# Holding DVE, ACT and POOL in the written order in the prompt-in, latents-out and prompt-out stages, and loading nine instead of five gated blocks early

## The chip, the core and the metric

The kernel runs on one core of one Trainium2 chip. The core has five engines with a queue of instructions each: TensorE (PE in the profile, with its weight loads as PEld), VectorE (DVE), ScalarE (ACT), GpSimd (POOL) and SyncE (SP), which here issues nearly all DMAs. [...] The metric is the device time of one execution in microseconds (us), as the median of several runs.

## The reference

One layer of a diffusion and flow-matching backbone is applied to two groups of tokens: 256 prompt tokens and 1024 latent tokens, of width 1024, in float32. Every step is modulated by vectors from a conditioning matrix product (`w_ada`).

```python
def swiglu(h, w_in, w_out):
    gate, up = jnp.split(h @ w_in, 2, axis=-1)
    return (jax.nn.silu(gate) * up) @ w_out
...
    h = rms_norm(x, p['norm_ffn1']) * (1.0 + sc1) + sh1
    x = x + 0.5 * g1 * swiglu(h, p['w_ffn1_in'], p['w_ffn1_out'])
    h = rms_norm(x, p['norm_mix']) * (1.0 + sc2) + sh2
    mix, k_ctx, v_ctx, s_ctx = token_mix(h, p, lb, lam_init, ctx_cache, rope)
    x = x + g2 * mix
    h = rms_norm(x, p['norm_ffn2']) * (1.0 + sc3) + sh3
    x = x + 0.5 * g3 * swiglu(h, p['w_ffn2_in'], p['w_ffn2_out'])
```

`token_mix` holds a gated linear recurrence and a differential attention. The two feed-forward networks (FFN1 and FFN2, inner width 2816 = 22 x 128) are what the change touches, with the first steps of the norms between them.

## The kernel before

**Matrix products.** Every float32 operand is split into two parts: a rounded high part (ACT, `copy`) and the rest (`tensor_tensor` with subtract, on DVE or POOL). A product is three matmuls: high by high, high by low, low by high. The tokens stand in three chunks: `CH[0]` and `CH[1]` of 512 latents each and `CH[2]` of 256 prompt tokens. For the latents the products of the FFNs use a seven-product scheme (Strassen with Winograd's sums) over quarters of the operands, so that sums of blocks have to be formed on DVE first.

**Stages of an FFN** (`ffn` in `build`), in order:

- `prompt_in`: the prompt tokens' gate and up products, 22 pairs of units of 24 matmuls. After each unit the next weight is split (`ahead(3)`: three units ahead, from four buffers) and `tick()` lets each generator in the list `side` take one step. There the latents' norms and their operands for the seven products (`operands`) are made, one step for each tick.
- `latents_in`: 11 x 2 x 7 products of the latents; gated blocks go to DRAM (`g_d`).
- `latents_out`: seven passes in the order `OUT = (1, 2, 5, 6, 7, 3, 4)`, each over 11 pairs of blocks: a weight block `b` and a gated block `g` of 128 x 512. `out_blocks` makes them: `self.block(a, .., G)` is an ACT cast and a POOL subtraction, `self.block(g, .., V)` an ACT cast and a DVE subtraction. In passes 5, 6, 7 and 3 a DVE sum comes first and the cast of `b` reads it. `pop(3)` makes blocks three ahead of the one in use; `wh` and `wl` have four buffers. After each block's 12 matmuls comes `tick()`: `drain` adds a pass's results into x (two `scalar_tensor_tensor` for each step; 16, 4, 8, 12, 8, 4 and 4 of them for the seven passes in order), and `later` takes one sum of squares for the next norm.
- `prompt_out`: 22 steps of 24 matmuls, two ticks for each; in FFN1 the norms of the two latent chunks (`norm` with `step=1`) run in its ticks.

**What sets the order.** The instructions are written in the order of the generators, and a planner then chooses each engine's order by its own estimate of when each instruction is ready; what is written first has priority. `keep_in_program_order` (line 51) takes that freedom away: an instruction it is called on stays behind the one written before it on the same engine. `nc.pin(names)` switches this on for the engines named and `nc.pin()` off. Before the change it is on only in attention (line 1681, for PE, DVE and ACT).

**Early loads.** `out_resident` loads weight blocks and five gated blocks (`g1`) into the space of the latents' operands (tags `hh0`, `hl0`, `hl1`), while `latents_in` ends. The gated blocks from the sixth on come through tag `gr` of the pool `op`, which takes the space of the pool `fp` of `latents_in`. Tags `hh2` and `hl2` hold the operand `t2` until the last product that reads it; then `out_resident` uses them for weights of pass 2.

Of the kernel before, what the change touches and what calls it, by code (L numbers as in the profile page):

```python
# [9 lines left out]
F32 = mybir.dt.float32  # L10
# [8 lines left out]
P = 128  # L19
# [14 lines left out]
def sub(a, off, dims):  # L34
    return bass.AP(tensor=a.tensor, offset=a.offset + off,
                   ap=[list(a.ap[0])] + [list(d) for d in dims])
# [29 lines left out]
class Kern:  # L66
# [9 lines left out]
    def pool(self, name, space=None, side=None):  # L76
        kw = {} if space is None else {"space": space}
        if space != DRAM:
            kw["reuse_waits"] = "tile"
        if side is not None:  # L80
            kw["side"] = side
        return self.tc.tile_pool(name=name, bufs=1, **kw)
# [273 lines left out]
    def rstd(self, tp, c, which, ms, lag):  # L356

        nc = self.nc
        n = CH[c][1]
        nt = n // P  # L360
        if ms is not None:
            nc.vector.tensor_tensor(ms[:, 0, :nt], ms[:, 0, :nt], ms[:, 1, :nt], op=ALU.add)
            ms = ms[:, 0]
        else:
            for _ in range(lag):
                yield
            acc, self.acc[c] = self.acc[c], {}
            ms = self.bank(f"pm{which}_{c}", nt)
            for t in range(nt):
                for h in range(2):  # L370
                    nc.tensor.matmul(ms[:, t:t + 1], acc[h][:, t * P:(t + 1) * P], self.ones[:, 0:1],
                                     start=h == 0, stop=h == 1)
        m = tp.tile([P, 4], F32, tag="nm", bufs=2, name=f"nm{which}_{c}")
        nc.vector.tensor_scalar(m[:, :nt], ms[:, :nt], 1.0 / D, EPS, op0=ALU.mult, op1=ALU.add)
        r = tp.tile([P, 4], F32, tag="nr", bufs=2, name=f"nr{which}_{c}")
        nc.gpsimd.tensor_tensor(r[:, :nt], m[:, :nt], self.nh[:, :nt], op=ALU.pow)
        dg = tp.tile([P, nt, P], F32, tag="t", bufs=self.tb, name=f"ndg{which}_{c}")
        nc.vector.tensor_tensor(dg, sub(self.ident, 0, [(0, nt), (1, P)]),
                                sub(r, 0, [(1, nt), (0, P)]), op=ALU.mult)
        yield  # L380
        if which:
            yield
        rb = self.bank(f"rb{which}_{c}", n)
        nc.tensor.matmul(rb, self.ones, dg.rearrange("p a b -> p (a b)"), start=True, stop=True)
        self.rb = rb
# [277 lines left out]

    def out_resident(self, hp, wout, name):

        t = [hp.tile([P, m, 512], F32, tag=g, name=f"{name}q{g}")
             for m, g in ((8, "hh0"), (8, "hl0"), (4, "hh2"), (2, "hl2"), (8, "hl1"))]
        fl = [x[:, j] for x, m in zip(t, (8, 8, 4, 2)) for j in range(m)]
        self.a11, self.a12 = fl[:NPR], fl[NPR:]
        self.s3, self.g1 = [t[4][:, j] for j in range(3)], [t[4][:, j] for j in range(3, 8)]  # L670
        for p in range(8):
            self.out_w(wout, self.a11[p], p, 0, 0)
            if p < 5:
                self.nc.sync.dma_start(self.g1[p], self.g_d[:, 0, p])

    def out_w(self, wout, t, p, i, j):
        self.nc.sync.dma_start(t, wout[0, (2 * p + j) * P:(2 * p + j + 1) * P, i * 512:(i + 1) * 512])
# [11 lines left out]
    def out_blocks(self, wout, name, hp, xp, pool):  # L689

        nc = self.nc
        V, G = nc.vector, nc.gpsimd
        keys = [(i, p) for i in self.OUT for p in range(NPR)]
        raws = {}
        xs = deque(self.x_pieces(xp))

        def load(j):
            if j >= len(keys):
                return
            i, p = keys[j]  # L700
            n_ = f"{name}w{i}_{p}"
            if j < 5:
                g = self.g1[j]
            else:
                g = pool().tile([P, 512], F32, tag="gr", bufs=4, name=n_ + "gr")
                nc.sync.dma_start(g, self.g_d[:, i - 1, p])
            a = None
            if i == 1:
                if p >= 8:
                    self.out_w(wout, self.a11[p], p, 0, 0)  # L710
            elif i == 2:
                self.out_w(wout, self.a12[p], p, 0, 1)
            elif i in (5, 7, 4):
                a = self.raw(pool, [P, 2, 512], n_ + "r")
                if i in (5, 7):
                    self.out_w(wout, a[:, 0], p, 1, 0)
                if i in (5, 4):
                    self.out_w(wout, a[:, 1], p, 1, 1)
            if xs and j >= 2 and j % 2 == 0:
                nc.sync.dma_start(*xs.popleft())  # L720
            if i == 5 and p == 4:
                self.x_move(pool(), 2, True)
            raws[j] = g, a
        s_ = None
        load(0)
        load(1)
        for j, (i, p) in enumerate(keys):
            load(j + 2)
            g, a = raws.pop(j)
            n_ = f"{name}w{i}_{p}"  # L730
            if i == 5 and p == 0:
                s_ = hp.tile([P, 8, 512], F32, tag="hh1", name=f"{name}s")
                s_ = [s_[:, q] for q in range(8)] + self.s3
            if i == 1:
                a = self.a11[p]
            elif i == 2:
                a = self.a12[p]
            elif i == 5:
                V.tensor_tensor(s_[p], a[:, 0], a[:, 1], op=ALU.add)
                a = s_[p]  # L740
            elif i == 6:
                V.tensor_tensor(s_[p], s_[p], self.a11[p], op=ALU.subtract)
                a = s_[p]
            elif i == 7:
                V.tensor_tensor(self.a11[p], self.a11[p], a[:, 0], op=ALU.subtract)
                a = self.a11[p]
            elif i == 3:
                V.tensor_tensor(self.a12[p], self.a12[p], s_[p], op=ALU.subtract)
                a = self.a12[p]
            else:  # L750
                a = a[:, 1]
            yield self.block(a, n_ + "b", G), self.block(g, n_ + "g", V)
# [747 lines left out]
def build(tc, ins, outs):  # L1500
    K = Kern(tc, ins, outs)
    nc = K.nc
# [4 lines left out]
    def mix_units():  # L1507
        K.tok_units(512, "hi0")
        for hd in range(4):
            K.hgrn_units(hd)  # L1510
            for w in MIX[hd]:
                K.tok_units(COL[w[0]] + 256 * int(w[1]), w)

    def ffn(st, name, which, hp, xp, side, nxt, done):

        win, wout = ins[f"w_{name}_in"], ins[f"w_{name}_out"]
        pool = {}
        ai, pi = K.stream(K.in_blocks(win, name, lambda: pool["fp"]))
        ao, po = K.stream(K.out_blocks(wout, name, hp, xp, lambda: pool["op"]))
        ap_, pp = K.stream(K.prompt_out_blocks(wout, name, lambda: pool["op"]))  # L1520

        def after():
            K.out_resident(hp, wout, name)
            ao(2)
        K.half = True
        K.xraw, K.nraw = st["raw"](), 3
        K.prompt_in(st["t"], name)
        K.finish_all()
        K.half = False
        K.xraw, K.nraw = None, 1  # L1530
        ai(1)
        st["close"]()
        with K.pool(name + "fp", side=side) as fp:
            pool["fp"] = fp
            st["side"]()
            K.latents_in(fp, name, pi, after)
            K.finish_all()
        st["end"]()
        with K.pool(name + "op", side=side) as op:
            pool["op"] = op  # L1540
            K.tb = 8
            m = 3 * which + 2
            K.latents_out(name, po, K.mt[m], K.ng[m], lambda c, d: done(op, c, d), lambda: ap_(2))
            K.prompt_out(name, pp, K.mt[m], lambda c, d: done(op, c, d))
            nxt(op)

    with ExitStack() as top:
# [7 lines left out]
        hp = top.enter_context(K.pool("h"))  # L1555
        K.ffn_units(ins["w_ffn1_in"], "ffn1")
        with K.pool("xx", side="right") as xp:
# [61 lines left out]
            def nxt(op):  # L1619
                mix_units()  # L1620
                K.ahead(2)
                ap = pv.enter_context(K.pool("pv"))
                K.att_consts(cp, ap)
                K.proj_v(ap, 0)
                K.finish_all()
                pv.close()
            ffn({"t": qp, "raw": lambda: qp, "close": q1.close, "side": lambda: K.side.append(adas()), "end": ta.close},
                "ffn1", 0, hp, xp, "right", nxt, done1)
        K.tb = 7
# [7 lines left out]
        for hd in range(4):  # L1637
            q = K.hgrn_q(gp, hd)
# [5 lines left out]
            for w in MIX[hd]:  # L1644
                g = int(w[1])
# [33 lines left out]
        with K.pool("atp", side="right") as atp, K.pool("psS", PSUM) as psS:  # L1679
# [3 lines left out]
            rest = [g for pr in (2, 3) for g in [K.proj_pair(avs[1][:2], *K.proj_av(att, 1), pr)] * 2]  # L1683
# [86 lines left out]
```

## Time and profile before

| what | us |
|---|---|
| runs (3), median | 2815.34 (2814.02 to 2816.27) |
| the profiled execution | 2819.1 |
| its span, first to last instruction | 2817.0 |
| PE busy | 2699.1 |
| DVE busy | 1666.7 |
| POOL busy | 1274.2 |
| ACT busy | 1116.4 |

The stages as the trace shows them, from the span's start: prompt-in of FFN1 to 193, its latents-in to 664, its latents-out 664 to 898, its prompt-out 898 to 978; the mixing to 1951; prompt-in of FFN2 to 2087, its latents-in to 2513, its latents-out 2513 to 2746, its prompt-out to 2811.

How to read it: every row has a start and a length, the engine, the operation with its tiles (`ffn1w_5g` is the split of gated block 5, `ffn1w_5b` that of weight block 5, `ffn1w_5gr` the raw gated block), and in brackets the idle time before and what ended it. A stage in which PE is busy all the time is bounded by PE; elsewhere the bracket names the engine that was late. All instructions are recorded by one helper (line 49), so the tile names tell them apart.

### The profile page before, as it was taken

Reading aid. Unit: us, or ns where it says so; the run is one execution under the profiler, and the core shown is the slowest. Engines: PE = TensorE matmul, PEld = TensorE weight load, DVE = VectorE, ACT = ScalarE, POOL = GpSimd, SP = SyncE. Lnnn points to the kernel's source line nnn. Section 1 sums busy time; section 2 is a strip of 40 time slices with the busy share of each in tenths; the row PEclk is TensorE's granted clock in tenths of the full one; section 3 lists DMA queues with packets and bytes.
Section 4 is the critical chain, followed back from the end, with each engine's and each line's share of the span. In section 5 each row is a group of like instructions: output and inputs, shape, how many; then the busy total and the mean of one; then the engine's idle time right before and its main releaser. Section 6 shows DMA issues by size and latency. Waiting matters only on the chain.

```text
span 2817.0 us, 43935 instructions
## 1 busy us (share of the span) xinstructions
PE 2699.1 (96%) x17070; PEld 2342.9 (83%) x17070; DVE 1666.7 (59%) x2158; ACT 1116.4 (40%) x1896; POOL 1274.2 (45%) x902
## 2 busy tenths in 40 slices
PE   7999999999899999999999899999999999999999
PEld 6986668887688889898989888888997888877789
DVE  3954446555876626464555488836745555557754
ACT  4642223333345523232323477745533333324344
POOL 2344334443545636455654112165454444435443
PEclk8999999999999999999999999999999999999999
DMA  9766663327635531313223954385653333257455
GB/s 302 232 187 213 203 203 121 106 83 242 231 119 187 175 123 58 109 61 101 67 81 99 224 116 104 121 282 162 187 150 102 96 102 113 94 190 253 135 178 185
DMA packets 412244, 429.29 MB, mean 152 GB/s; under 512 B 20620, under 2 KB 314756, under 8 KB 409988
## 3 DMA queue, kind: packets, MB, share of 16 engines
q1 hardware_dynamic: 411856, 426.43, 48.8%
q8 instruction: 134, 2.20, 0.3%
q14 instruction: 74, 0.61, 0.1%
q10 hardware_dynamic: 180, 0.06, 0.0%
HBM read 326.79 MB, written 99.61 MB: 151 GB/s over the span
## 4 chain that ended last, share of the span: by engine, by line
PE 80%; DVE 9%; DMA 4%; issue 3%; POOL 3%; SPq 1%; ACT 1%; ACTq 0%; DVEq 0%; POOLq 0%
PE ffn2po L49 6%; PE ffn1po L49 5%; PE mob L49 4%; PE ffn2pp L49 2%; PE ffn2pu L49 2%; PE ffn2pg L49 2%; PE ffn1pg L49 2%; PE ffn1pu L49 2%; PE ffn1pp L49 1%; PE ada L49 1%; PE ak1b L49 1%; PE ak0b L49 1%; PE aq0b L49 1%; SPq L49 1%; PE av1b L49 1%
## 5 line engine op out<-in xcount | busy, mean ns | idle before, releaser
L49 PE MATMUL ffn1pp<-ffn1pvv,ffn1pw 128*128 128x256 f32 x528 | 70.3, 296 | 5.6 <-DVE ffn1pvv L49 4.7
L49 PEld LDWEIGHTS ffn1pp<-ffn1pvv,ffn1pw 128*128 128x128 f32 x528 | 68.3, 203 | 7.5 <-DVE ffn1pvv L49 5.5
L49 PE MATMUL ffn2pp<-ffn2pvv,ffn2pw 128*128 128x256 f32 x528 | 64.0, 283 | 0.0
L49 PEld LDWEIGHTS ffn2pp<-ffn2pvv,ffn2pw 128*128 128x128 f32 x528 | 63.6, 192 | 0.1
L49 POOL TENSOR_TENSOR ffn2pw<-ffn2pw,ffn2pw 128x512 fp32r<-128x512 f32 x22 | 28.9, 1316 | 35.8 <-ACT ffn2pw L49 35.8
L49 PE MATMUL ada<-wada,cst 128*32 128x256 f32 x448 | 39.5, 391 | 0.6 <-DMA wada<-w_ada 0.5
L49 POOL TENSOR_TENSOR hl<-nt,hh 128x256 fp32r<-128x256 f32 (+1 forms) x20 | 22.3, 1119 | 39.0 <-ACT hh L49 36.6
L49 POOL TENSOR_TENSOR ffn1pw<-ffn1pw,ffn1pw 128x512 fp32r<-128x512 f32 x22 | 33.0, 1508 | 14.1 <-ACT ffn1pw L49 14.0
L49 ACT ACTIVATE nt<-nt,mt,sv 128x256 f32<-128x256 f32 (+1 forms) x40 | 25.7, 680 | 30.3 <-DVE sv L49 18.1
L49 DVE TENSOR_TENSOR sacc<-sacc,sq 128x512 f32<-128x512 f32 (+1 forms) x18 | 29.4, 1632 | 10.9 <-ACT sq L49 10.6
L49 PE MATMUL ffn1po<-ffn1w_5g,ffn1w_5b 128*128 128x512 f32 x84 | 24.4, 446 | 9.2 <-ACT ffn1w_5g L49 5.2
L49 ACT CAST ffn2pw<-ffn2pw 128x512 fp32r<-128x512 f32 x44 | 26.9, 620 | 15.5 <-PE ffn2pp L49 8.9
L49 ACT CAST ffn1pw<-ffn1pw 128x512 fp32r<-128x512 f32 x44 | 26.1, 616 | 16.3 <-DMA ffn1pw<-w_ffn_out 10.8
L49 DVE TENSOR_TENSOR ffn2pw<-ffn2pw,ffn2pw 128x512 fp32r<-128x512 f32 x22 | 16.9, 766 | 25.9 <-ACT ffn2pw L49 25.9
L49 PEld LDWEIGHTS ffn1po<-ffn1w_5g,ffn1w_5b 128*128 128x128 f32 x84 | 18.3, 220 | 14.1 <-ACT ffn1w_5g L49 5.6
L49 DVE TENSOR_REDUCE a_0mx<-a_0S 128x1 f32<-128x1536 f32 x8 | 14.1, 1757 | 24.3 <-PE a_0S L49 24.2
L49 PEld LDWEIGHTS ada<-wada,cst 128*32 128x32 f32 x448 | 9.6, 108 | 22.1 <-issue 19.5
L49 PE MATMUL ffn2po<-ffn2w_5g,ffn2w_5b 128*128 128x512 f32 x84 | 22.5, 421 | 5.6 <-ACT ffn2w_5g L49 5.6
L49 DVE TENSOR_TENSOR ffn1pw<-ffn1pw,ffn1pw 128x512 fp32r<-128x512 f32 x22 | 17.9, 816 | 13.2 <-ACT ffn1pw L49 13.2
L49 POOL TENSOR_TENSOR sacc<-sacc,sq 128x512 f32<-128x512 f32 (+1 forms) x18 | 25.0, 1392 | 0.5
L49 PEld LDWEIGHTS ffn2po<-ffn2w_5g,ffn2w_5b 128*128 128x128 f32 x84 | 17.0, 206 | 9.6 <-ACT ffn2w_5g L49 6.0
L49 PE MATMUL ffn2po<-ffn2w_9g,ffn2w_9b 128*128 128x512 f32 x84 | 22.0, 412 | 2.8 <-DVE ffn2w_9g L49 2.8
(4066 smaller groups left out, 10304.9 us busy)
## 6 DMA issues: line engine op xcount, KB each, us to landing
wada<-w_ada SPq DMA_DIRECT2D x112, 256.0 KB, 2.9
ffn1r<-w_ffn_in SPq DMA_DIRECT2D x44, 512.0 KB, 4.3
ffn2r<-w_ffn_in SPq DMA_DIRECT2D x44, 512.0 KB, 4.0
ffn1pw<-w_ffn_out SPq DMA_DIRECT2D x22, 512.0 KB, 3.4
ffn2pw<-w_ffn_out SPq DMA_DIRECT2D x22, 512.0 KB, 3.4
g_d<-ffn1t SPq DMA_DIRECT2D x33, 256.0 KB, 2.9
g_d<-ffn2t SPq DMA_DIRECT2D x33, 256.0 KB, 3.0
wadb<-w_ada SPq DMA_DIRECT2D x12, 512.0 KB, 9.1
```

Of the source, the lines that this page charges most:

```text
L49: r = f(*a, **k)
```

## The change

Three edits. `nc.pin("vector", "scalar", "gpsimd")` is switched on around `prompt_in` and around `latents_out` and `prompt_out` of both FFNs. `rstd` gets two more `yield`s: one between the row sums on PE and the DVE instruction that reads them, one (for the second and third norm) between the power on POOL and the DVE instruction that reads that; so each norm takes two ticks more. `out_resident` loads gated blocks 0 to 8 instead of 0 to 4, the four new ones into `hh2`; the last six weight blocks of pass 2, which had that space, get their tiles later (`rest12`, called in pass 2 at block 5).

```diff
@@ -370,10 +370,13 @@
                     nc.tensor.matmul(ms[:, t:t + 1], acc[h][:, t * P:(t + 1) * P], self.ones[:, 0:1],
                                      start=h == 0, stop=h == 1)
+            yield
         m = tp.tile([P, 4], F32, tag="nm", bufs=2, name=f"nm{which}_{c}")
         nc.vector.tensor_scalar(m[:, :nt], ms[:, :nt], 1.0 / D, EPS, op0=ALU.mult, op1=ALU.add)
         r = tp.tile([P, 4], F32, tag="nr", bufs=2, name=f"nr{which}_{c}")
         nc.gpsimd.tensor_tensor(r[:, :nt], m[:, :nt], self.nh[:, :nt], op=ALU.pow)
+        if which:
+            yield
         dg = tp.tile([P, nt, P], F32, tag="t", bufs=self.tb, name=f"ndg{which}_{c}")
@@ -663,15 +666,23 @@
     def out_resident(self, hp, wout, name):
 
-        t = [hp.tile([P, m, 512], F32, tag=g, name=f"{name}q{g}")
-             for m, g in ((8, "hh0"), (8, "hl0"), (4, "hh2"), (2, "hl2"), (8, "hl1"))]
-        fl = [x[:, j] for x, m in zip(t, (8, 8, 4, 2)) for j in range(m)]
+        def tile_(m, g, n="q"):
+            return hp.tile([P, m, 512], F32, tag=g, name=f"{name}{n}{g}")
+        t = [tile_(8, "hh0"), tile_(8, "hl0"), None, None, tile_(8, "hl1")]
+        fl = [x[:, j] for x in t[:2] for j in range(8)]
         self.a11, self.a12 = fl[:NPR], fl[NPR:]
-        self.s3, self.g1 = [t[4][:, j] for j in range(3)], [t[4][:, j] for j in range(3, 8)]
+        g = tile_(4, "hh2", "g")
+        self.g1 = [t[4][:, j] for j in range(3, 8)] + [g[:, j] for j in range(4)]
+
+        def rest():
+            t = tile_(4, "hh2"), tile_(2, "hl2")
+            self.a12 += [x[:, j] for x, m in zip(t, (4, 2)) for j in range(m)]
+        self.rest12 = rest
+        self.s3 = [t[4][:, j] for j in range(3)]
         for p in range(8):
             self.out_w(wout, self.a11[p], p, 0, 0)
-            if p < 5:
-                self.nc.sync.dma_start(self.g1[p], self.g_d[:, 0, p])
+            self.nc.sync.dma_start(self.g1[p], self.g_d[:, 0, p])
+        self.nc.sync.dma_start(self.g1[8], self.g_d[:, 0, 8])
@@ -699,7 +710,9 @@
             i, p = keys[j]
             n_ = f"{name}w{i}_{p}"
-            if j < 5:
+            if i == 2 and p == 5:
+                self.rest12()
+            if j < 9:
                 g = self.g1[j]
@@ -1524,8 +1537,10 @@
         K.xraw, K.nraw = st["raw"](), 3
+        nc.pin("vector", "scalar", "gpsimd")
         K.prompt_in(st["t"], name)
         K.finish_all()
+        nc.pin()
@@ -1540,8 +1555,10 @@
             m = 3 * which + 2
+            nc.pin("vector", "scalar", "gpsimd")
             K.latents_out(name, po, K.mt[m], K.ng[m], lambda c, d: done(op, c, d), lambda: ap_(2))
             K.prompt_out(name, pp, K.mt[m], lambda c, d: done(op, c, d))
+            nc.pin()
             nxt(op)
```

## The prediction

> **What bounds the kernel now.** I read the first table of the page, then busy time by stage, then PE's own timeline in the pinned stages, then the timelines of DVE, ACT and POOL around each idle time of PE.
>
> ```profile
> span 2817.0 us, 43935 instructions
> PE 2699.1 (96%) x17070; PEld 2342.9 (83%) x17070; DVE 1666.7 (59%) x2158; ACT 1116.4 (40%) x1896; POOL 1274.2 (45%) x902
> 55.77:193.00 137.23, 128.79 (x1018) 125.96 (x1018) 97.50 (x118) 81.19 (x135) 56.33 (x24) 0.96 0.73 219
> 658.50:980.00 321.50, 299.22 (x1536) 255.75 (x1535) 237.12 (x285) 145.09 (x260) 168.17 (x116) 0.97 0.59 194
> 1955.00:2112.00 157.00, 151.98 (x1150) 145.27 (x1148) 95.15 (x105) 72.81 (x106) 73.70 (x35) 0.99 0.59 170
> 2507.00:2730.00 223.00, 210.39 (x932) 172.77 (x931) 162.06 (x189) 86.91 (x153) 106.82 (x73) 0.98 0.60 195
> ```
>
> The last four rows are stretches: its bounds, its length, the busy time (and instructions) of PE, PEld, DVE, ACT and POOL, the granted clock, the DMA share, GB/s. PE is busy 96% of the span, so only its idle time and its slow clock can be won; whatever starves it is lost in full. In the four stages (prompt-in of FFN1, the out stages of FFN1, prompt-in of FFN2, latents-out of FFN2) its idle time is 8.4, 22.3, 5.0 and 12.6 us: some 48 us is the most that order can give, a little more with the clock that comes back late after a stop. In latents-out the idle time stands in two places.
>
> ```profile
> 658.77 0.39 PE L49 MATMUL ffn1u10p<-o0t2hh,ffn1w101s 128*128 128x512 f32 x1
> ...
> 675.31 2.88 PE L49 MATMUL ffn1po<-ffn1w_4g,ffn1w_4b 128*128 128x512 f32 x12
> ...
> 683.37 4.56 PE L49 MATMUL ffn1po<-ffn1w_5g,ffn1w_5b 128*128 128x512 f32 x12 [5.17 <-ACT ffn1w_5g L49]
> 687.76 2.90 PE L49 MATMUL ffn1po<-ffn1w_6g,ffn1w_6b 128*128 128x512 f32 x12
> ...
> 742.19 0.61 PE L49 MATMUL ffn1po<-ffn1w_4g,ffn1w_4b 128*128 128x512 f32 x2
> 746.04 2.56 PE L49 MATMUL ffn1po<-ffn1w_4g,ffn1w_4b 128*128 128x512 f32 x10 [3.23 <-POOL ffn1w_4b L49]
> 752.87 5.06 PE L49 MATMUL ffn1po<-ffn1w_5g,ffn1w_5b 128*128 128x512 f32 x11 [4.04 <-DVE ffn1w_5g L49]
> ...
> 777.23 0.39 PE L49 MATMUL ffn1po<-ffn1w_1g,ffn1w_1b 128*128 128x512 f32 x1
> ```
> ```profile
> 2523.94 2.88 PE L49 MATMUL ffn2po<-ffn2w_4g,ffn2w_4b 128*128 128x512 f32 x12
> 2532.44 4.99 PE L49 MATMUL ffn2po<-ffn2w_5g,ffn2w_5b 128*128 128x512 f32 x12 [5.61 <-ACT ffn2w_5g L49]
> 2537.26 2.88 PE L49 MATMUL ffn2po<-ffn2w_6g,ffn2w_6b 128*128 128x512 f32 x12
> ...
> 2586.22 0.39 PE L49 MATMUL ffn2po<-ffn2w_2g,ffn2w_2b 128*128 128x512 f32 x1
> ...
> 2593.79 2.98 PE L49 MATMUL ffn2po<-ffn2w_4g,ffn2w_4b 128*128 128x512 f32 x12
> ...
> 2619.53 2.91 PE L49 MATMUL ffn2po<-ffn2w_10g,ffn2w_10b 128*128 128x512 f32 x12
> ```
>
> Blocks that don't wait start 2.72 us apart. Blocks 4 and 5 of pass 1 take 687.76 - 675.31 = 12.45 us in FFN1 and 13.32 in FFN2, where two cost 5.44: 7.0 and 7.9 us are lost at gated block 5. In pass 5 eight blocks take 35.0 us in FFN1 (742.19 to 777.23) and 33.3 in FFN2, of which two groups of transposes take 1.6; eight cost 21.8: 13.3 and 10.0 us are lost while the planner has put sums for later passes ahead of the splits that PE needs.
>
> **The change part by part.**
>
> *Gated blocks.* Block 5 is late because its load comes so late:
>
> ```profile
> 656.47 2.22 SPq L49 DMA_DIRECT2D ffn1qhl<-g_d  x5
> ...
> 677.78 0.43 SPq L49 DMA_DIRECT2D ffn1w_5gr<-g_d  x1
> ```
>
> The five early loads issue at 656.47, the sixth only at 677.78. After the change blocks 5 to 8 load into `hh2`, whose last reader (t2) starts at 658.77, and block 9 is the first to wait for the pool: issued as late as block 5 was and landed 4.9 us later with its cast (682.70), it is needed only at 683.37 - 5.17 + 4 x 2.72 = 689.1. So -7.0 and -7.9. The same loads move forward on SP; weight blocks 6 and 7 queue behind them for at most 3 us and are needed after 680. `rest12` waits for gated blocks 5 to 8, used up a pass earlier: nothing.
>
> *The tail in front.* The first pinned DVE instruction (the split of gated block 2) now stands behind the last one of latents-in. That run of operations (the first and the last row), and PE's block 2:
>
> ```profile
> 663.80 0.68 DVE L49 TENSOR_TENSOR ffn1u10y<-ffn1u10x,ffn1u10p 128x512 f32<-128x512 f32 x1
> ...
> 675.75 0.68 DVE L49 TENSOR_TENSOR ffn1g10x<-ffn1t,ffn1g10z 128x512 f32<-128x512 f32 x1
> 669.87 2.88 PE L49 MATMUL ffn1po<-ffn1w_2g,ffn1w_2b 128*128 128x512 f32 x12
> ```
>
> From 663.80 twelve operations at 0.60 (one behind the other) end at 671.0, with one that meets POOL at 672; then the split, 0.69. PE wants it at 669.87: 1.8 to 2.9 us late, I take 2.5 for each FFN: +5.0.
>
> *Written order in passes 5, 6, 7 and 3.* For each block DVE's order is now: sum, split of `g`, two drains if there are any, next sum. The cast of `b` waits for the sum, the cast of `g` stands behind it on ACT, and DVE's split waits for that: a closed chain, where now the sums lie far ahead. Its pieces, from a steady stretch:
>
> ```profile
> 791.97 0.62 ACT L49 CAST ffn1w_9b<-ffn1qhl 128x512 fp32r<-128x512 f32 x1 [1.58 <-PE ffn1po L49]
> 792.49 0.62 ACT L49 CAST ffn1w_9g<-ffn1w_9gr 128x512 fp32r<-128x512 f32 x1
> 792.66 1.29 POOL L49 TENSOR_TENSOR ffn1w_9b<-ffn1qhl,ffn1w_9b 128x512 fp32r<-128x512 f32 x1 [1.42 <-ACT ffn1w_9b L49]
> 793.14 1.36 DVE L49 TENSOR_TENSOR ffn1w_9g<-ffn1w_9gr,ffn1w_9g 128x512 fp32r<-128x512 f32 x1 [1.35 <-ACT ffn1w_9g L49]
> 799.87 2.88 PE L49 MATMUL ffn1po<-ffn1w_9g,ffn1w_9b 128*128 128x512 f32 x12
> 755.14 0.68 DVE L49 TENSOR_TENSOR ffn1s<-ffn1s,ffn1qhh 128x512 f32<-128x512 f32 x1
> 779.95 2.06 DVE L49 SCALAR_TENSOR_TENSOR xr1a<-ffn1po,mt,xr1a 128x512 f32<-128x512 f32 x3
> ```
>
> From the start of `b`'s cast to the end of `g`'s split: 794.50 - 791.97 = 2.53 us; the split takes 1.36 instead of 0.69 because POOL's subtraction of `b` started before it. The sum adds 0.68 and a hand-over of some 0.05, less 0.1 by which successive DVE operations overlap: 3.15 us for each block against PE's 2.72. A drain adds 0.66 (three take 2.06). Behind the waiting split stand those drains and the next sum; ACT's next cast waits for the sum and PE for the split, so nothing runs ahead. For the 44 blocks: 44 x 3.15 = 138.6, and 32 drains (4, 8, 12, 8) x 0.66 = 21.1, together 159.7 against 44 x 2.72 = 119.7 us of PE: 40 too many. The start is covered: block 9 is ready at 794.50 and used at 799.87, 5.4 us of lead. So 34.6 us lost in FFN2; in FFN1 three POOL additions for the norm add 1.3 each, 38.5. Against 10.0 and 13.3 now that is +24.6 and +25.2. The trace doesn't show this chain closed, so bounds: drains hidden in the waits, 13.5 lost (44 x 0.43 - 5.4); no meeting with POOL, 5 lost; neither hidden and no lead, 44.
>
> *Prompt-in.* The same kind of chain stands in four of 22 steps (`operands`, c = 1): DVE difference, ACT cast, DVE split, twice, then the weights' split, then two more differences and a split.
>
> ```profile
> 109.24 0.69 DVE L49 TENSOR_TENSOR o0b<-x1b,o0a 128x512 f32<-128x512 f32 x1
> 110.78 1.22 DVE L49 TENSOR_TENSOR ffn1g10l<-ffn1g10r,ffn1g10h 128x1024 fp32r<-128x1024 f32 x1
> 165.71 2.41 POOL L49 TENSOR_TENSOR ffn1u18l<-ffn1u18r,ffn1u18h 128x1024 fp32r<-128x1024 f32 x1 [3.74 <-ACT ffn1u18h L49]
> ```
>
> Four waits for a cast and seven operations at 0.6, the weights 1.2 and 0.3 for the gate make 7.3 us for a step, and 8.8 if a POOL split (2.41) falls on DVE's work; PE needs 5.8. Four steps lose 6 to 12, less some 3 of lead: 3 to 9, I take 6 in each FFN. Idle now is 8.4 and 5.0: -2 and +1, with 2 more in FFN1 as my estimate for the slow clock behind its stops (-4), together -3; bounds -13 and +8.
>
> *Prompt-out and the yields.* In FFN1 the latents' norms run there:
>
> ```profile
> 900.00:910.00 10.00, 9.08 (x76) 8.87 (x75) 10.00 (x15) 7.59 (x15) 6.18 (x4) 1.00 0.63 226
> 930.00:940.00 10.00, 8.18 (x61) 7.58 (x62) 10.00 (x14) 7.83 (x17) 7.63 (x5) 1.00 0.44 127
> ```
>
> DVE is busy all the time here; the same work in another order ends no sooner. I put 0, with bounds of -8 (PE idles 2.74 us in these 20, so some 6 in the 43 us of the norms, and 2 in a stop near the stage's end) and +8 (half of the 16 steps wait 1 us for ACT). The yields move each norm back by two ticks, under 6 us, in stages where its reader comes later: 0.
>
> The sum: -14.9 + 5.0 + 49.8 - 3 + 0 = +36.9 us on the profiled execution's 2819.1 (span 2817.0 and 2.1 around it): 2856. The median lies 3.8 lower: 2852.
>
> **The rivals.**
>
> *The chain stays open (faster).* If the split doesn't meet POOL, a block costs 3.15 - 0.67 = 2.48 us, less than PE's 2.72, and only the drains are over: 109.1 + 21.1 - 119.7 - 5.4 = 5.1 lost, 9.0 in FFN1. The sum is -14.9 + 5.0 - 9.2 - 3 = -22, and -30 with prompt-out's 8: 2785 to 2793. It decides at 2.72 us for a block. For it: with a sum of DVE in front, POOL's timing may shift. Against it: all the steady splits in this stretch show 1.36. [...]
>
> *Drains hidden (no change).* They fall into waits for ACT: 13.5 and 17.4 lost, +7.6 instead of +49.8: 2810.
>
> *The clock falls (slower still).* PE now stops at every block.
>
> ```profile
> 750.00:760.00 10.00, 7.13 (x20) 5.68 (x21) 9.97 (x14) 1.14 (x2) 3.54 (x3) 0.66 0.46 141
> 760.00:770.00 10.00, 9.63 (x42) 7.31 (x40) 10.00 (x11) 3.56 (x7) 5.13 (x4) 1.00 0.52 175
> 973.26 4.51 PE L49 MATMUL ffn1pp<-ffn1pvv,ffn1pw 128*128 128x256 f32 x23 [2.07 <-DVE ffn1pvv L49]
> ```
>
> At a granted clock of 0.66 a block takes 4.1 us, the chain's mean is 3.63: 44 x 0.49 = 21.6 more in each FFN, 2895. For it: 0.66 after a stop of 4 us, and a slow restart after one of 2.07. Against it: 1.00 in 760 to 770, where PE still idles a little. [...]
>
> *The pins don't hold*: then only the gated blocks are left, -15: 2800.
>
> **How the numbers follow.** Forecast, the chain closed: 0.62, own range 2828 to 2880. Open chain: 0.19. Pins don't hold: 0.03. Drains hidden: 0.08. Clock falls: 0.08. A measurement tells about 0.2% from no change, 5.6 us. Slower 0.70, same 0.08, faster 0.22. The range 2786 to 2885 leaves out half of the faster cases and most of the clock's.
>
> **What would show it.** Right: PE's blocks in passes 5, 6, 7 and 3 start 3.1 us and more apart, some 4.5 with drains, each idle time ended by DVE's split of `g`; each cast of `b` right behind its sum; no stop at gated block 5, one of 2 to 3 us at block 2. Wrong: blocks at 2.72 in passes 6 and 7, or sums several blocks ahead of their casts.

## The result: slower by 3.46%, and the profile after

| | us |
|---|---|
| before, median of 5 runs in the comparison | 2815.34 (2811.69 to 2818.96) |
| after, median of 5 runs | 2912.24 (2909.93 to 2915.48) |
| ratio after to before | 1.0346, 95% interval 1.0334 to 1.0358 |
| forecast | 2852.0, range 2786 to 2885 |

The kernel became slower, as forecast, but by 96.9 us and not by 36.9: the time lies outside the range. The profiled execution's span went from 2817.0 to 2908.2, 91.2 us more; the profiled run of before lies 3.8 us above its median and that of after 2.3 below. First, busy time by stage, before and then after. A stage here goes from its first matmul to the first of the next one; the rows are prompt-in, latents-out and prompt-out of FFN1, prompt-in and latents-out of FFN2, with the columns as in the prediction (bounds, length, busy time of PE, PEld, DVE, ACT and POOL, granted clock, DMA share, GB/s).

```profile
35.00:192.70 157.70, 144.84 (x1124) 141.09 (x1125) 104.52 (x126) 92.15 (x154) 65.39 (x28) 0.95 0.75 222
664.40:897.80 233.40, 218.49 (x944) 178.00 (x943) 172.10 (x197) 95.99 (x170) 118.45 (x84) 0.98 0.59 195
897.80:977.80 80.00, 72.63 (x549) 70.67 (x548) 60.80 (x83) 45.78 (x86) 49.07 (x31) 0.94 0.55 181
1950.90:2086.30 135.40, 131.14 (x1075) 129.41 (x1074) 81.22 (x93) 67.44 (x95) 57.61 (x24) 0.99 0.62 183
2513.10:2745.50 232.40, 219.79 (x973) 180.56 (x972) 166.86 (x196) 91.43 (x162) 113.15 (x77) 0.98 0.60 195
```
```profile
34.90:207.80 172.90, 148.88 (x1124) 143.59 (x1125) 109.94 (x123) 91.61 (x154) 63.24 (x28) 0.92 0.66 203
679.60:940.30 260.70, 230.92 (x941) 172.29 (x941) 181.34 (x194) 94.22 (x168) 113.06 (x85) 0.99 0.53 173
940.30:1037.30 97.00, 77.57 (x550) 73.39 (x549) 66.18 (x86) 49.67 (x90) 47.18 (x33) 0.89 0.44 151
2008.40:2152.50 144.10, 135.24 (x1075) 133.53 (x1074) 91.08 (x104) 71.36 (x105) 59.26 (x25) 0.95 0.58 172
2580.20:2836.60 256.40, 230.55 (x973) 174.82 (x972) 178.54 (x195) 90.88 (x162) 101.21 (x78) 1.00 0.55 176
```

The five stages grew by 15.2, 27.3, 17.0, 8.7 and 24.0 us: 92.2, which is all of it (the rest fell by about 1). The two latents-out stages grew by 51.3, by the chain that was forecast; the forecast gave them +39.9 (-14.9 + 5.0 + 49.8). The two prompt-in stages and the prompt-out stage were forecast at -3 together and grew by 40.9: there the prediction failed. PE's busy time grew too, by 4.0, 4.9 and 4.1 us in the three prompt stages, with a granted clock of 0.92, 0.89 and 0.95 instead of 0.95, 0.94 and 0.99: the same matmuls ran longer behind the stops (a clock of 0.66 from 68 to 73 us, behind the first stop at `rb`; 0.50 from 956.3 to 964.3 in prompt-out; 0.50 from 2062.4 to 2068.4 in FFN2).

**Latents-out.** PE's own timeline in pass 6 of FFN1, first without drains, then with two drains for each block:

```profile
789.08 2.79 PE L49 MATMUL ffn1po<-ffn1w_2g,ffn1w_2b 128*128 128x512 f32 x11 [0.23 <-DVE ffn1w_2g L49]
792.33 2.79 PE L49 MATMUL ffn1po<-ffn1w_3g,ffn1w_3b 128*128 128x512 f32 x11 [0.23 <-DVE ffn1w_3g L49]
...
796.87 2.83 PE L49 MATMUL ffn1po<-ffn1w_4g,ffn1w_4b 128*128 128x512 f32 x11 [0.88 <-DVE ffn1w_4g L49]
...
801.42 2.79 PE L49 MATMUL ffn1po<-ffn1w_5g,ffn1w_5b 128*128 128x512 f32 x11 [0.88 <-DVE ffn1w_5g L49]
```

The blocks stand 3.25 us apart (792.33 - 789.08) and 4.55 with two drains (801.42 - 796.87); without a wait they stand 2.72 apart. Each stop ends with DVE's split of `g`. The engines beside it, from one block to the next (rows of the timeline of all engines, here and below in order of time):

```profile
789.74 0.62 ACT L49 CAST ffn1w_3b<-ffn1s 128x512 fp32r<-128x512 f32 x1 [2.10 <-DVE ffn1s L49]
...
790.26 0.62 ACT L49 CAST ffn1w_3g<-ffn1w_3gr 128x512 fp32r<-128x512 f32 x1
...
790.44 1.29 POOL L49 TENSOR_TENSOR ffn1w_3b<-ffn1s,ffn1w_3b 128x512 fp32r<-128x512 f32 x1 [1.96 <-ACT ffn1w_3b L49]
...
790.91 1.36 DVE L49 TENSOR_TENSOR ffn1w_3g<-ffn1w_3gr,ffn1w_3g 128x512 fp32r<-128x512 f32 x1 [1.28 <-ACT ffn1w_3g L49]
...
792.20 1.40 DVE L49 SCALAR_TENSOR_TENSOR xr1a<-ffn1po,mt,xr1a 128x512 f32<-128x512 f32 x2
...
793.52 0.67 DVE L49 TENSOR_TENSOR ffn1s<-ffn1s,ffn1qhh 128x512 f32<-128x512 f32 x1
...
794.30 0.62 ACT L49 CAST ffn1w_4b<-ffn1s 128x512 fp32r<-128x512 f32 x1 [3.42 <-DVE ffn1s L49]
```

Read in order of time: cast of `b` at 789.74, cast of `g` behind it, POOL's split of `b` at 790.44, DVE's split of `g` at 790.91 with 1.36 us because POOL started first (in e4, where DVE's split of `4g` comes first, it takes 0.68), two drains, the next sum at 793.52, and only then ACT's next cast of `b` (794.30), after 3.42 us of waiting for DVE. It is the closed chain.

**Prompt-out of FFN1**, where the latents' norms run in the ticks: PE, then DVE over one step.

```profile
986.61 0.74 PE L49 MATMUL ffn1pp<-ffn1pvv,ffn1pw 128*128 128x256 f32 x4 [1.49 <-ACT ffn1pvv L49]
988.94 2.65 PE L49 MATMUL ffn1pp<-ffn1pvv,ffn1pw 128*128 128x256 f32 x20 [1.59 <-DVE ffn1pvv L49]
993.09 0.74 PE L49 MATMUL ffn1pp<-ffn1pvv,ffn1pw 128*128 128x256 f32 x4 [1.50 <-ACT ffn1pvv L49]
```
```profile
988.81 1.27 DVE L49 TENSOR_TENSOR nt<-xr0b,rb 128x512 f32<-128x512 f32 x2
991.73 0.89 DVE L49 CAST hh<-nt 128x512 fp32r<-128x512 f32 x1 [1.65 <-ACT nt L49]
992.65 0.69 DVE L49 TENSOR_TENSOR hl<-nt,hh 128x512 fp32r<-128x512 f32 x1
993.26 1.76 DVE L49 TENSOR_TENSOR ffn1pw<-ffn1pw,ffn1pw 128x512 fp32r<-128x512 f32 x1
```

A step takes 993.09 - 986.61 = 6.48 us; its 24 matmuls take 3.39 (0.74 + 2.65). DVE multiplies two rows of the norm, then waits 1.65 us for ACT to scale and shift the second one, and only behind that cast and split does it come to the weights' split, which PE needs. Over the part of the stage in which the norms run, first before and then after (columns as in the stretches above):

```profile
897.80:939.00 41.20, 36.40 (x265) 34.91 (x264) 40.30 (x55) 29.30 (x55) 26.13 (x18) 0.92 0.47 156
940.30:1000.00 59.70, 43.70 (x288) 39.94 (x287) 43.05 (x58) 31.92 (x57) 24.60 (x19) 0.89 0.36 124
```

DVE was idle for 0.90 us of it (41.20 - 40.30) and is now for 16.65 (59.70 - 43.05). Nine waits for ACT's work on the norms make up 15.1 us of that; six of them are the wait of 1.65.

**Prompt-in.** In FFN1 PE stops at the broadcast of the norm (`rb`), in FFN2 at the weights of the steps in which the operands are made:

```profile
64.98 2.34 POOL L49 TENSOR_TENSOR ffn1u4l<-ffn1u4r,ffn1u4h 128x1024 fp32r<-128x1024 f32 x1
...
65.05 2.82 DVE L49 TENSOR_TENSOR ndg<-ident,nr 128x512 f32<-128x512 f32 x1 [1.13 <-POOL nr L49]
...
68.02 1.43 PE L49 MATMUL rb<-ndg,ones 128*128 128x512 f32 x2 [4.58 <-DVE ndg L49]
```
```profile
103.20 2.04 PE L49 MATMUL rb<-ndg,ones 128*128 128x512 f32 x2 [6.01 <-DVE ndg L49]
...
2060.22 2.84 POOL L49 TENSOR_TENSOR ffn2u8l<-ffn2u8r,ffn2u8h 128x1024 fp32r<-128x1024 f32 x1 [7.75 <-ACT ffn2u8h L49]
...
2060.78 2.83 DVE L49 TENSOR_TENSOR o2b<-xr1b,o2b 128x512 fp32r<-128x512 f32 x1
...
2063.12 0.58 PE L49 MATMUL ffn2pu<-hh,ffn2u8l 128*128 128x256 f32 x1 [2.42 <-POOL ffn2u8l L49]
...
2072.53 0.39 PE L49 MATMUL ffn2pu<-hh,ffn2u9l 128*128 128x256 f32 x1 [0.91 <-POOL ffn2u9l L49]
```

`ndg`, on which `rb` waits, takes 2.82 us, since POOL's split of the next weights started 0.07 us before it; in the two latents' norms PE stands still for 4.58 and 6.01 us. The meeting is 2.1 us of each (2.82 - 0.69). In FFN2 the steps with operands are 2072.53 - 2063.12 = 9.41 us long (the next two 9.38 and 9.40); the last DVE split of a step takes 2.83 us beside a POOL split that started 0.56 earlier.

### The profile page after: what moved, and what is told of

Read it like the earlier page. It is cut to its first block, busy times and chain, and to the rows that moved or that the text cites. A ratio compares the mean times of both kernels' runs of the same rounds, so it can differ in the third digit from the quotient of the medians.

```text
span 2908.2 us, 43948 instructions
## 1 busy us (share of the span) xinstructions
PE 2732.4 (94%) x17070; PEld 2337.6 (80%) x17070; DVE 1694.0 (58%) x2158; ACT 1113.1 (38%) x1896; POOL 1251.9 (43%) x902
## 5 line engine op out<-in xcount | busy, mean ns | idle before, releaser
L49 DVE TENSOR_TENSOR ffn2s<-ffn2s,ffn2pu 128x256 f32<-128x256 f32 x22 | 9.2, 416 | 42.5 <-PE ffn2pu L49 14.5
L49 DVE TENSOR_TENSOR ffn2pvv<-ffn2pv,ffn2pvv 128x256 fp32r<-128x256 f32 x22 | 12.8, 583 | 26.9 <-ACT ffn2pvv L49 26.5
L49 DVE TENSOR_TENSOR ffn1pw<-ffn1pw,ffn1pw 128x512 fp32r<-128x512 f32 x22 | 25.9, 1178 | 1.1 <-ACT ffn1pw L49 0.6
L49 PE MATMUL ffn1po<-ffn1w_6g,ffn1w_6b 128*128 128x512 f32 x84 | 21.8, 401 | 4.5 <-DVE ffn1w_6g L49 2.6
L49 PE MATMUL ffn1po<-ffn1w_2g,ffn1w_2b 128*128 128x512 f32 x84 | 22.5, 411 | 3.7 <-DVE ffn1w_2g L49 3.7
L49 PE MATMUL ffn1po<-ffn1w_7g,ffn1w_7b 128*128 128x512 f32 x84 | 21.8, 401 | 4.4 <-ACT ffn1w_7g L49 2.2
L49 PE MATMUL ffn2po<-ffn2w_6g,ffn2w_6b 128*128 128x512 f32 x84 | 21.9, 400 | 3.3 <-DVE ffn2w_6g L49 1.9
```

Source lines behind the costliest of these rows:

```text
L49: r = f(*a, **k)
```

## The experiments

All lengths by stage are from the first matmul of a stage to the first of the next, to within 0.2 us, in the profiled execution of each kernel (us):

| kernel | median | prompt-in 1 | latents-out 1 | prompt-out 1 | mixing | prompt-in 2 | latents-out 2 |
|---|---|---|---|---|---|---|---|
| before | 2815 to 2817 | 157.7 | 233.4 | 80.0 | 973.1 | 135.4 | 232.5 |
| after | 2912.2 | 172.9 | 260.7 | 97.0 | 971.0 | 144.1 | 256.4 |
| e1, gates alone | 2802.1 | 154.0 | 226.5 | 77.5 | 973.1 | 136.2 | 224.5 |
| e2, held in latents-out alone | 2876.2 | 155.7 | 260.0 | 79.5 | 978.4 | 135.5 | 257.1 |
| e3, sums one ahead | 2830.8 | 176.5 | 215.6 | 97.0 | 973.9 | 144.1 | 217.4 |
| e4, DVE alone held | 2835.5 | 161.8 | 228.3 | 94.9 | 981.5 | 141.9 | 224.3 |
| e8, ACT alone held | 2799.1 | 154.7 | 224.3 | 81.9 | 970.7 | 134.2 | 224.3 |
| e5, e3 + norms and operands ahead | 2815.8 | 169.9 | 217.3 | 91.3 | 973.8 | 139.8 | 218.0 |
| e9, e5 + weights split on POOL | 2815.9 | 167.4 | 214.0 | 87.6 | 976.5 | 139.8 | 217.6 |
| e6, e3 + rb later, hold later | 2813.4 | 164.2 | 211.3 | 95.9 | 971.6 | 144.1 | 214.8 |
| e10, all held, e3 + e5 + e6 | 2797.4 | 155.5 | 211.3 | 92.8 | 974.3 | 139.7 | 214.8 |
| e7, e2 + sums ahead, hold later | 2781.3 | 155.9 | 211.3 | 78.0 | 979.0 | 135.5 | 214.8 |

Prompt-in of FFN1 moves by up to 4 us between kernels that leave it alone, and the mixing by some 10: both are left out of the readings below where a difference is that small.

### e1: the nine gated blocks alone

```diff
-        nc.pin("vector", "scalar", "gpsimd")
         K.prompt_in(st["t"], name)
...
-            nc.pin("vector", "scalar", "gpsimd")
             K.latents_out(name, po, ...)
...
                                      start=h == 0, stop=h == 1)
-            yield
```

> The kernel before with the nine gated blocks alone: no engine held in the written order, no further yields. If the stop at gated block 5 comes from its late load alone, both stops (7.0 and 7.9 us) go and nothing else moves: 2815.3 - 14.9 = 2800. The rival: block 9 becomes the first late one and stops PE in its place, so that nothing is won: 2813 to 2817.

Measured: 2802.08, ratio 0.994 (0.9925 to 0.9955) to a before of 2816.94, so -14.9 us; latents-out 6.9 and 8.0 shorter. The stops at gated block 5 are gone and no other came in their place in pass 1. The term holds.

### e2: held in latents-out alone

```diff
-        nc.pin("vector", "scalar", "gpsimd")
         K.prompt_in(st["t"], name)
         K.finish_all()
-        nc.pin()
...
             K.latents_out(name, po, ...)
+            nc.pin()
             K.prompt_out(name, pp, ...)
-            nc.pin()
```

> The changed kernel, with the three engines held in the written order in latents-out alone (prompt-in and prompt-out are left to the planner; nine gates and yields stay). If each stage loses by its own written order, prompt-in gives back 15.1 + 8.7 us and prompt-out of FFN1 17.1: 2912.2 - 40.9 = 2871, with the out stages as long as in the changed kernel (260.7 and 256.4 us). The rival: the added yields, not the held order, cost the 17.1 us in prompt-out, which then stay: 2888.

Measured: 2876.24, ratio 1.0204 (1.0187 to 1.0221). Both prompt-in stages and prompt-out are back at their lengths of before (155.7, 135.5, 79.5) with the yields still in: the held order costs the 17 us there, the yields nothing. Latents-out stays as long as after the change. That the median is 5 above the forecast is the mixing (978.4), whose cause is not known.

### e3: the sum written one block ahead

```diff
             load(j + 2)
-            g, a = raws.pop(j)
+            while len(made) < min(2, len(keys) - j):
+                made.append(summed(j + len(made)))
+            a = made.popleft()
+            g, _ = raws.pop(j)
```

(`summed(j)` holds the lines that form block j's sum, unchanged.)

> The changed kernel with one thing moved in the written order: the DVE sum of a block is written one block ahead, before the split of the block in front of it. If the loss in passes 5, 6, 7 and 3 is the closed chain (sum, cast of b, cast of g, split), it opens: ACT's next cast of b no longer waits for the split. DVE then has 0.68 + 1.36 us for a block and 0.66 for each of 32 drains, a mean of 2.52 against PE's 2.72, so the blocks without drains stand 2.72 apart and most of 2 x 28 us goes: 2855 to 2865. The rival: DVE's meetings with POOL set the pace, not the chain; then the blocks stay 3.25 and 4.55 apart and the time stays within 5 us of 2912.

Measured: 2830.84, ratio 1.0043 (1.0027 to 1.0059): 81 us less than the change, and more than forecast. PE, ACT and DVE in pass 7 of this kernel:

```profile
802.50 0.68 DVE L49 TENSOR_TENSOR ffn1qhh<-ffn1qhh,ffn1w_1r 128x512 f32<-128x512 f32 x1
...
802.51 2.88 PE L49 MATMUL ffn1po<-ffn1w_8g,ffn1w_8b 128*128 128x512 f32 x12
...
802.75 0.62 ACT L49 CAST ffn1w_0b<-ffn1qhh 128x512 fp32r<-128x512 f32 x1 [1.58 <-POOL ffn1w_10b L49]
...
803.92 1.37 DVE L49 TENSOR_TENSOR ffn1w_0g<-ffn1w_0gr,ffn1w_0g 128x512 fp32r<-128x512 f32 x1 [0.75 <-ACT ffn1w_0g L49]
...
805.23 1.07 PE L49 MATMUL ffn1po<-ffn1w_9g,ffn1w_9b 128*128 128x512 f32 x4
```

The blocks stand 2.72 apart through all four passes, those with drains too (where transposes stand between them in FFN2 apart), though the split still takes 1.37 beside POOL. The sum at 802.50 is that of block 1 (it reads `1r`), while ACT has still to cast `0b`: the cast no longer waits for the newest sum. It seems to come as PE uses up blocks: its bracket names POOL's split of `10b`, but that had ended at 802.03, and the same wait of 1.58 before `8b`, `9b` and `10b` is put down to PE. So the chain set the pace; a meeting with POOL alone does not. More came back than forecast, because 2 x 28 us was the growth against the kernel before: against 2.72 us for each of 44 blocks the four passes had lost 44.4 and 41.9 us in the changed kernel, and now lose nothing in FFN1 and 3.6 in FFN2, which are the transposes.

### e4 and e8: one engine held

```diff
-nc.pin("vector", "scalar", "gpsimd")
+nc.pin("vector")
```

> The changed kernel with DVE alone held in the written order; ACT and POOL are the planner's. The closed chain needs both: ACT's cast of g behind the cast of b, and DVE's next sum behind the split of g. If ACT may cast g first, the split no longer waits for the sum: the out stages fall back from 260.7 and 256.4 us to about 235, some 45 us less, about 2865. The rival: DVE's order alone does the harm (whatever waits on it is late whichever way ACT goes); then 2895 to 2912.

> The changed kernel with ACT alone held in the written order. If the chain needs DVE's held order as much as ACT's, the planner puts the sums far ahead as before the change, the casts find them ready and the out stages come near those with the nine gates alone (226.5 and 224.5): about 2805. The rival: ACT's order alone, cast of g behind cast of b, does the harm: 2860 and more.

(e8 has `nc.pin("scalar")`.) Measured: 2835.45, ratio 1.0065 (1.0046 to 1.0083), and 2799.13, ratio 0.9951 (0.9933 to 0.9968). With DVE alone held, latents-out falls to 228.3 and 224.3. ACT and DVE where the planner uses ACT's freedom, in pass 6:

```profile
774.50 0.62 ACT L49 CAST ffn1w_3g<-ffn1w_3gr 128x512 fp32r<-128x512 f32 x1
...
775.02 0.62 ACT L49 CAST ffn1w_4g<-ffn1w_4gr 128x512 fp32r<-128x512 f32 x1
...
775.15 1.36 DVE L49 TENSOR_TENSOR ffn1w_3g<-ffn1w_3gr,ffn1w_3g 128x512 fp32r<-128x512 f32 x1 [1.28 <-ACT ffn1w_3g L49]
...
778.35 0.68 DVE L49 TENSOR_TENSOR ffn1w_4g<-ffn1w_4gr,ffn1w_4g 128x512 fp32r<-128x512 f32 x1
...
778.52 0.62 ACT L49 CAST ffn1w_4b<-ffn1s 128x512 fp32r<-128x512 f32 x1 [2.88 <-DVE ffn1s L49]
```

Up to 774.50 ACT goes in the written order and the split takes 1.36; the blocks there are 3.25 apart. At 775.02 the cast of `4g` comes ahead of that of `4b`: in blocks 4 to 7 the split of `g` is done before POOL starts on `b`, takes 0.68, and PE's blocks stand 2.72 apart from block 5 to the end of the pass. Where ACT is back in the written order, as at the start of pass 7, they stand 3.25 apart again. With ACT alone held the stages are about those of the gates alone. The chain needs the held order of DVE and of ACT; what holding POOL adds was not run by itself. Prompt-in of FFN2 and prompt-out are long with DVE alone held (141.9 and 94.9) and short with ACT alone (134.2 and 81.9): there it is DVE's order that costs.

### e5 and e9: the norms and the operands

```diff
+            while len(made) < (2 if step == 1 and d < KD - 1 else 1):
+                e = d + len(made)
...
+                nc.vector.tensor_tensor(t, self.x[c][e], rb, op=ALU.mult)
+                nc.scalar.activation(t, t, AF.Identity, ...)
+                made.append(t)
+            t = made.popleft()
...
-            self.split(t1[0][:, d], t1[1][:, d], a)
...
             nc.vector.tensor_tensor(b, x1[4 + d], a, op=ALU.subtract)
+            self.split(t1[0][:, d], t1[1][:, d], a)
```

> The kernel of e3 with two more places of the written order changed, each in a stage of its own: in prompt-out's norms the product and the ACT step of row d+1 are written ahead of the casts and splits of row d; in prompt-in's operands the second DVE difference is written ahead of the split of the first. If prompt-out loses by DVE's wait for ACT's step (1.65 us in each of some 5 steps of 6.48), the stage falls from 97.0 to about 88; in prompt-in one of the waits of 0.69 goes in four steps, 144.1 to about 141 in FFN2. The rival: DVE's own work with its meetings with POOL sets both stages (about 4.9 and 8.7 us for a step without any wait), so that the waits only fill room: both within 1 us of e3.

> The kernel of e5 with the first weight split of each prompt-out step moved from DVE to POOL, which then makes both. In e5 the steps with a norm in prompt-out of FFN1 stand 5.79 us apart and PE needs some 3.2. If what is left there is DVE's own work in the held order, lengthened by its meetings with POOL (split of the weights 1.1 to 1.76, of the gated block 1.49 instead of 0.41), the steps shorten by the 1.1 to 1.76 that leave DVE, until POOL is the bound: two splits and one for the norm, 3.9 us without meetings and 5.1 with them. Prompt-out of FFN1 from 91.3 to 84 to 88. The rival: the wait for ACT's casts sets the steps, whoever splits; then 91 and more, and POOL late in the steps without a norm too.

Measured: 2815.84, ratio 0.9998 (0.9986 to 1.001), and 2815.94, ratio 0.9998 (0.9987 to 1.001). In e5 prompt-out of FFN1 fell by 5.7 us (9 forecast) and prompt-in of FFN2 by 4.3 (3 forecast). PE's timeline in prompt-out of e5 and of e9:

```profile
941.71 2.65 PE L49 MATMUL ffn1pp<-ffn1pvv,ffn1pw 128*128 128x256 f32 x20 [0.99 <-DVE ffn1pvv L49]
...
947.50 2.65 PE L49 MATMUL ffn1pp<-ffn1pvv,ffn1pw 128*128 128x256 f32 x20 [0.98 <-DVE ffn1pvv L49]
```
```profile
931.82 2.64 PE L49 MATMUL ffn1pp<-ffn1pvv,ffn1pw 128*128 128x256 f32 x20 [0.53 <-DVE ffn1pvv L49]
...
937.15 4.75 PE L49 MATMUL ffn1pp<-ffn1pvv,ffn1pw 128*128 128x256 f32 x25 [0.53 <-DVE ffn1pvv L49]
```

The steps went from 6.48 to 5.79 in e5 and to 5.33 in e9, where prompt-out fell by 3.7 us more. Both theories hold a part. In e5 DVE waits 0.35 us a step for ACT's row of the norm and 0.58 for its cast of the weights, together 0.93 instead of 1.65: 0.7 us less, as the step. In e9 the split of 1.1 has left DVE, but its waits for ACT are 0.35 and 1.40 (now for the cast of the gated block), 0.8 more than in e5, so that the step is only some 0.5 shorter. The 1.9 us that e9 still has over PE's 3.39 are PE's stops for ACT's cast of the gated block (1.42) and for DVE's split of it (0.53); no run takes them out.

### e6: rb one tick later, the hold from the second block on

```diff
         yield
-        if which:
+        if which or more:
             yield
         rb = self.bank(f"rb{which}_{c}", n)
...
+                if i == 1 and p == 1:
+                    nc.pin("vector", "scalar", "gpsimd")
                 w, v = pop(3)
```

(`more` is true for the latents' first norms.)

> The kernel of e3 with two edits: the broadcast of the latents' first norms (rb) is written one tick later, and the three engines are held in the written order from the second block of latents-out on, not from its start. If rb stands in PE's queue a tick too early for a DVE that is held in order, its two stops (4.48 and 6.02 us) go, and with them some 2 us of slow clock: prompt-in of FFN1 from 176.5 to about 164. If the split of block 2 is late because it stands behind the tail of latents-in, its stops (2.46 and 2.32 us) go too: latents-out 213 and 215 us. In all about 2815. The rival: the norm's result is late whenever it is asked for, so that the stops move to its readers, and block 2 waits for its load: 2830.

Measured: 2813.36, ratio 0.9994 (0.9982 to 1.0006). Prompt-in of FFN1 is 164.2, as forecast (8.7 us shorter than after the change, 12.3 than in e3): one stop at `rb` is 1.75 us, the other is gone. Latents-out is 211.3 and 214.8, and PE does not stop there at all: the stop at block 2 was the tail in front.

### e7 and e10: put together

e7 has the gates, the held order in latents-out alone and from its second block on, and the sums one block ahead. e10 holds all stages, as the change does, with the edits of e3, e5 and e6.

> What the stages so far suggest together: nine gated blocks; the three engines held in the written order in latents-out alone, from its second block on; the sums written one block ahead. From the stages: 2815.3 - (233.4 - 213.2) - (232.5 - 215.1) = 2778. The rival: prompt-in and prompt-out, left to the planner, or the mixing come out longer than before (they did by 5 us in e2): 2785.

> All three stages held in the written order as in the change, with every edit of that order from e3, e5 and e6 together: the sums one block ahead, the norm's rows one ahead, the operands' differences first, rb one tick later, the hold of latents-out from its second block on. If each closed a wait of its own, they add up: from e3 (2830.8) 12.3 for rb, 4.3 + 2.6 for block 2, 5.7 for the norms, 4.3 and some 4 for the operands: 2798, faster than before, though every stage is still held. The rival: the planner's freedom is worth something that no written order here gives back; the gains overlap and it stays at 2808 to 2815.

Measured: e7 2781.34 (2779.10 to 2786.73), ratio 0.9884 (0.9865 to 0.9903): faster than both kernels, by 34 us than before (2815.74 beside it) and by 131 than after. It lies between the two cases because the mixing is 979.0 instead of 973.1. e10: 2797.44, ratio 0.9928 (0.9911 to 0.9945), as forecast: the gains of the edits add up to within a few us in each stage. So most of the cost was not that the order was held but which order it was. Not all of it: with every edit prompt-out still takes 92.8 us against 80.0 before and prompt-in of FFN2 139.7 against 135.4, and e7, which leaves both to the planner, is 16 us faster than e10.

## Why the prediction was wrong

**Gated blocks, -14.9**: right. e1 gives -14.9.

**The tail in front, +5.0**: right in mechanism, too small; +8.2. Blocks 2 of the first passes:

```profile
686.63 1.63 DVE L49 TENSOR_TENSOR ffn1g10x<-ffn1t,ffn1g10z 128x512 f32<-128x512 f32 x1
...
688.92 3.45 PE L49 MATMUL ffn1po<-ffn1w_2g,ffn1w_2b 128*128 128x512 f32 x9 [3.00 <-DVE ffn1w_2g L49]
...
2589.47 2.33 PE L49 MATMUL ffn2po<-ffn2w_2g,ffn2w_2b 128*128 128x512 f32 x9 [2.96 <-DVE ffn2w_2g L49]
```

The stops are 3.00 and 2.96 us, where 1.8 to 2.9 were forecast: two of the tail's operations met POOL in each FFN (1.67 and 1.63 us instead of 0.68), where one was counted. With the slow clock behind the first (0.66 from 689 to 694 us), pass 1 of FFN1 lost 4.9 us there (blocks 2 and 3 from 685.08 to 695.47, less 5.44) and that of FFN2 3.3 (2585.66 to 2591.64, less 2.72).

**Written order in passes 5, 6, 7 and 3, +49.8**: right; +58.8. A block took 3.25 us (forecast 3.15), a drain 0.65 (4.55 - 3.25, halved; forecast 0.66). From the first block of pass 5 to that of pass 4, FFN1 went from 133.8 us (731.31 to 865.15) to 164.1 (744.43 to 908.54) and FFN2 from 133.0 (2580.78 to 2713.82) to 161.6 (2643.32 to 2804.93). In the forecast's own sum 0.10 us more in each of 88 blocks are 8.8 of the 9.0 by which the term was too small. The first blocks of pass 5 still start 2.72 apart, on the lead that the sum allowed for; in passes 6 and 7 what would have shown it wrong, blocks at 2.72 or sums several blocks ahead of their casts, is not there. The rival of the hidden drains fell, and so did that of the falling clock: between these stops it was granted in full (1.00 over the four passes, 744.43 to 908.54 and 2643.32 to 2804.93 us).

**Prompt-in, -3 (bounds -13 and +8)**: wrong; +23.9. Two things went wrong in the step. It priced the operands' chain at 7.3 us for a step, 8.8 with a meeting; it measured 9.41, since the meeting at its end costs 2.83 - 0.69 = 2.1 us and not 1.5 (7.3 + 2.1 = 9.4; the 7.3 comes out though the step has two waits of 0.69 for a cast, where four were counted), and the slow clock behind the new stops was not in the sum. And it counted only the operands: the norms of the same generator, held in the same order, were left out. By the rows of the result, 10.6 of the 23.9 us are the two stops at `rb`, 8.1 the busy time that PE gained at the slower clock (4.0 + 4.1), and 5.2 other idle time. The stops at `rb` and the clock behind them are most of the 15.2 us in FFN1: with `rb` later the stage is 8.7 us shorter than after the change and 12.3 shorter than in e3, which the edit starts from (e6).

**Prompt-out, 0 (bounds -8 and +8)**: wrong; +17.0. The step read: DVE is busy all the time here, the same work in another order ends no sooner. That is true and says nothing of how much later it ends. A DVE without idle time has no room to take in a wait: the held order put 15.1 us of waits for ACT in its way, and PE's idle time over the same part grew from 4.80 to 16.00 us. The bound of +8 took a wait of 1 us in half of the 16 steps; six waits of 1.65 and three others came, and PE's matmuls ran 4.9 us longer at the slower clock. Where e5 took 0.7 us of wait out of a step, the step became 0.7 us shorter. By e2 and e8 the stage is back at 79.5 and 81.9 as soon as DVE may go on with other work.

**The yields, 0**: right, by e2.

**The sum.** On the profiled executions: -14.9 for the gates, some +8 for the tail, +58.8 for the four passes, +23.9 and +17.0 for the prompt stages, about -2 elsewhere: +91. The forecast had the sign and the largest term. Of the 54 us that it lacked, 43.9 are the prompt stages (40.9 and the -3), 9.0 the pace of the blocks and 3 the tail: the steps that failed are those that put prompt-in at -3, without the norms, and prompt-out at 0.

## What to carry to other kernels

When an engine's order is fixed, go through the written order of every stage it covers and look for an instruction that waits for another engine which in its turn waits for something written behind it; each such round trip can become the stage's pace, and an engine that was busy all the time before is the one that can least take it in. Writing the producer one step ahead was worth 81 us here; holding that stage alone, from its second block on, another 49. Read a stop's price with the clock behind it: three stages lost 4 to 5 us each to matmuls that ran slow behind their stops.

## What the runs showed of the hardware

Stops of PE of nearly the same length were not followed by the same clock. The granted clock behind the stops at block 2 of FFN1 (3.00 us) and FFN2 (2.96 us), behind a stop of 2.46 us in e3 (block 2 of FFN1, the third row), and in pass 6 of FFN1 after the change, where PE stops for 0.23 us at each block:

```profile
689.00:694.00 5.00, 5.00 (x15) 3.94 (x16) 2.04 (x4) 1.14 (x2) 0.84 (x1) 0.66 0.96 288
2589.50:2594.50 5.00, 5.00 (x22) 4.15 (x23) 3.08 (x4) 1.14 (x2) 1.29 (x1) 1.00 0.95 307
695.40:700.40 5.00, 5.00 (x15) 3.97 (x16) 1.74 (x3) 1.01 (x2) 0.31 (x1) 0.66 0.97 302
783.00:793.00 10.00, 9.31 (x39) 6.72 (x38) 6.15 (x8) 3.43 (x6) 3.88 (x3) 1.00 0.28 79
```

The third figure from the end is the clock, a mean over the stretch: 0.66, 1.00, 0.66 and 1.00. Before the first two of these stops PE ran without another (blocks 0 and 1, 679.64 to 685.08 and 2580.22 to 2585.66, start 2.72 us apart). So the length of a stop alone does not tell here which clock follows: behind 3.00 and 2.46 us it was 0.66, behind 2.96 us 1.00. What else decides it no run of this case shows. Not expected either was how much the meeting with POOL cost `ndg`, which started 0.07 us behind POOL's split: it took 2.82 us and ended 0.55 us after that split (64.98 + 2.34), where the kernel before had

```profile
62.42 0.69 DVE L49 TENSOR_TENSOR ndg<-ident,nr 128x512 f32<-128x512 f32 x1 [0.43 <-POOL nr L49]
```

with POOL idle beside it.
